# Four-layer, two-block forward pass: TensorE in source order at the norms, wider FFN opening tiles, urgent FFN adds, a norm mean in two steps

## Chip, cores and metric

One core of one Trainium2 chip runs the whole program. The time is the device time of one execution in microseconds (us); lower is better.

## What is computed

256 tokens of width 1024 go through a first block of two layers and a second block of two layers, all in float32. Written short, with the parts that the change touches:

```python
def mla_mixer(q_lat, kv_lat, k_rope, cos, sin, q_norm, kv_norm, w_uq, w_ukv, w_o):
    ...
    return o.reshape(bsz, s, MLA_WIDTH) @ w_o
def swiglu_ffn(h, w_gate_up, w_down):
    gt, up = jnp.split(h @ w_gate_up, 2, axis=-1)
    return (jax.nn.silu(gt) * up) @ w_down
def rmsnorm(x, g):
    y = x * lax.rsqrt(jnp.mean(x * x, axis=-1, keepdims=True) + 1e-6)
    return y * g
# first block, twice (l = 0, 1):
h = rmsnorm(x, norm_mix[l])
u, q_lat, kv_lat, k_rope, hq, hf, hi, hg, gate_logits = split(h @ w_in[l])
merged = sum over branches of sigmoid(gates[b]) * y_b      # b: s5, mla, hgrn2
x = x + merged @ w_out[l]
x = x + memory_cross_attention(rmsnorm(x, norm_cross[l]), rmsnorm(mem, norm_mem[l]), ...)
x = x + swiglu_ffn(rmsnorm(x, norm_ffn[l]), ffn_w_gate_up[l], ffn_w_down[l])
# then rmsnorm(x, norm_final), and the second block, twice:
y = concat(windowed_attention(...), rmsnorm(diff_attention(...), subln[l]))   # from rmsnorm(x, g_attn[l])
x = x + y @ w_out_2[l]
h = rmsnorm(x, g_ffn[l])
gate, val = split(h @ w_up_2[l]);  gate = conv3_over_tokens(gate)
x = x + (silu(gate) * val) @ w_down_2[l]
```

The FFN width is 2816, that is 22 pairs of 128 gate columns and 128 value columns. The MLA mixer has eight heads with keys of 96 rows (64 without and 32 with rotation).

## The kernel before

**Precision and weights.** Every product of float32 matrices is three matmuls: high times high, high times low and low times high part (`mm3`, lines 295 to 297). One such triple is called a step below. A weight tile of 128 by 1024 comes in by one 512 KB DMA on the SP queue into one of four raw buffers (`wload`, line 287), ACT copies its high part (`wh`, line 237), and DVE subtracts it from the raw tile to get the low part (`wl`, line 225).

**Who orders the work.** Each engine takes its instructions in one fixed order. The tile framework's scheduler makes that order from the source and from priorities: what stands under `urgent()` is put ahead of other work that is ready. `pe_order()` marks a stretch in which PE keeps the order of the source.

**Tokens and norms.** The 256 tokens are two tiles (t = 0, 1) of 128. The residual stream `x` is kept with tokens on partitions. A norm of class `Norm` runs per tile in this chain: the residual add of a PSUM half on DVE (line 225, `x<-x,ps`), the squares with their row sums on ACT (line 412, recorded at 237, `xs<-x`), after the second half the sum of both row sums on POOL (line 422), the mean on POOL (line 423), the power of minus one half on POOL (line 428), the scaling on DVE (line 234, `xs<-x,sm,g`, twice 512 columns), and then eight PE transposes (line 268, `ps<-con,xs`), whose results ACT and DVE split into the high and low part of `hh`, on which the next projection runs. `trans_split` (line 378) is the transposes with the split. The norms are the two of each layer's mixer and FFN, and the cross norm. `NormLate` and `Norm2` transpose the gained input before the root mean square is known, so that no transpose waits for the power.

**Projections.** `proj_a` keeps tokens on PSUM partitions; with `by_t` tile 0 is done wholly before tile 1. `proj_resid` adds a projection into the residual stream, then calls the next norm's squares and its power per tile. Where its weights have two k-groups (w_xo) it runs tile by tile and half by half, 12 matmuls of 512 columns for each.

**FFN** (`ffn`, line 1361). `head` (line 1376) does the first two gate/value pairs tile by tile: for each tile and pair 24 matmuls of 256 columns, 96 in an FFN. The other 20 pairs run with weights as the stationary operand and all 256 tokens moving: matmuls of 512 and 256 columns (`mm_both`, lines 378 to 381, `ps<-hh,wh`), then an ACT copy and a DVE add of the two PSUM halves (lines 1420 and 1421, recorded at 237 and 225, `UT<-ps,UT` and `MG<-ps,MG`). The down products of a pair follow three pairs later; the last four come tile by tile at the end, with the next norm's chain (lines 1428 to 1437).

**First mixer.** In layer 0 the constants of the S5 mixer are made beside the projections (`s5_prep`): DVE writes `PH` (line 225, `PH<-ST`), PE transposes it (line 268, `ps<-con,PH`), and ACT computes sines and exponentials, which need different tables (`ACT_TABLE_LOAD`). The FFN of layer 0 has the same preparation for layer 1 as its side work (on DVE `GT<-...`, `W<-...`, `Q<-...` and others, 896 columns).

**MLA scores.** `mla_attn` (line 1072) multiplies the rows 0 to 95 of `Q` and `K`.

## Time and profile before

| | |
|---|---|
| three runs | 1724.74, 1730.53, 1730.77 us, median 1730.53 us |
| the profiled execution | 1727.87 us, span 1725.8 us |
| TensorE clock granted over the span | 0.998 of full speed |
| PE | 1664.7 us busy (96 %), 9256 matmuls |
| DVE | 1326.3 us (77 %), 2474 instructions |
| ACT | 1008.1 us (58 %), 1790 instructions |
| POOL | 115.6 us (7 %), 174 instructions |
| chain that ended last | PE 73 %, DVE 11 %, ACT 8 %, issue 3 %, POOL 2 %, DMA 2 % |

The profiled execution lies 2.66 us under the median of the runs. In a row of the trace the first number is the start in us from the span's start, the second the duration; the name left of `<-` is written, the names right of it are read; the number in brackets is how long the engine was idle just before, and what ended that. Matmuls overlap, so that a row's duration is longer than the distance to the next one. A row with xN stands for N instructions of one form.

### The profile page before, as it was taken

What the parts mean: (1) busy time and instruction counts of PE and PEld (TensorE: products, weight loads), DVE (VectorE), ACT (ScalarE), POOL (GpSimd) and SP (SyncE); (2) the same over time, 40 slices, a digit from 0 to 9 for tenths busy, and PEclk for the clock granted to TensorE, in tenths of its full rate; (3) what the DMA queues carried; (4) which work ended last, traced back from release to release, by engine and by line L of the source; (5) the groups of instructions that cost most, each with busy time, mean ns of one, the idle gap of its engine ahead of it and who ended that gap; (6) DMA issues with size and microseconds to landing.
All of it is one profiled execution on the core that took longest, in us unless ns stands there. A gap on an engine that the chain in (4) does not pass through costs nothing.

```text
span 1725.8 us, 25598 instructions
## 1 busy us (share of the span) xinstructions
PE 1664.7 (96%) x9256; PEld 1386.3 (80%) x9256; DVE 1326.3 (77%) x2474; ACT 1008.1 (58%) x1790; POOL 115.6 (7%) x174
## 2 busy tenths in 40 slices
PE   7999999998999999999999999989899999999999
PEld 6977777887888788878778888866788886678887
DVE  7988887758976778975666666788687787878776
ACT  5873455556665576354465555657566655756554
POOL 1010000010110100000000000221000003100000
PEclk9999999999999999999999999999999999999999
DMA  7675464646677456446554666543466654346664
GB/s 238 186 262 166 155 209 146 186 150 188 221 254 239 142 165 187 154 148 189 186 172 162 188 194 192 167 147 113 135 190 190 193 169 145 110 131 187 190 190 133
DMA packets 85088, 304.92 MB, mean 177 GB/s; under 512 B 9569, under 2 KB 10337, under 8 KB 84961
## 3 DMA queue, kind: packets, MB, share of 16 engines
q1 hardware_dynamic: 81792, 291.74, 54.3%
q0 software_dynamic: 3168, 11.54, 1.9%
q8 instruction: 73, 1.20, 0.3%
q14 instruction: 55, 0.44, 0.1%
HBM read 290.66 MB, written 12.58 MB: 176 GB/s over the span
## 4 chain that ended last, share of the span: by engine, by line
PE 73%; DVE 11%; ACT 8%; issue 3%; POOL 2%; DMA 2%; SPq 0%; POOLq 0%; ACTq 0%; DVEq 0%
PE ps L379 17%; PE ps L295 13%; PE ps L297 13%; PE ps L296 13%; PE ps L378 7%; PE ps L268 3%; DVE wl L225 3%; ACT wh L237 3%; DVE W L225 2%; PE ps L1187 1%; ACT W L237 1%; PE ps L381 1%; PE ps L937 1%; PE ps L1072 1%; DVE W L949 1%
## 5 line engine op out<-in xcount | busy, mean ns | idle before, releaser
L225 DVE TENSOR_TENSOR wl<-wr,wh 128x1024 fp32r<-128x1024 f32 (+2 forms) x516 | 618.7, 1203 | 166.5 <-ACT wh L237 164.5
L237 ACT ACTIVATE wh<-wr 128x1024 fp32r<-128x1024 f32 (+2 forms) x516 | 536.1, 1042 | 310.8 <-PE ps L297 203.7
L379 PE MATMUL ps<-hh,wh 128*128 128x512 f32 x1280 | 450.4, 397 | 2.9 <-DVE UT L225 2.7
L378 PE MATMUL ps<-hh,wl 128*128 128x256 f32 x1120 | 312.5, 279 | 0.7 <-DVE wl L225 0.7
L379 PEld LDWEIGHTS ps<-hh,wh 128*128 128x128 f32 x1280 | 234.4, 188 | 49.6 <-issue 3.2
L295 PE MATMUL ps<-wh,hh 128*128 128x512 f32 (+2 forms) x640 | 233.7, 367 | 4.2 <-ACT UT L237 3.9
L296 PE MATMUL ps<-wl,hh 128*128 128x512 f32 (+2 forms) x640 | 235.1, 368 | 2.3 <-DVE wl L225 2.2
L297 PE MATMUL ps<-wh,hh 128*128 128x512 f32 (+2 forms) x640 | 232.8, 364 | 0.0
L378 PEld LDWEIGHTS ps<-hh,wl 128*128 128x128 f32 x1120 | 211.2, 189 | 8.0 <-DVE wl L225 1.0
L295 PEld LDWEIGHTS ps<-wh,hh 128*128 128x128 f32 x640 | 121.4, 190 | 23.8 <-ACT UT L237 4.4
L296 PEld LDWEIGHTS ps<-wl,hh 128*128 128x128 f32 x640 | 121.6, 190 | 22.8 <-DVE wl L225 4.5
L297 PEld LDWEIGHTS ps<-wh,hh 128*128 128x128 f32 x640 | 121.7, 190 | 17.3 <-issue 1.0
L295 PE MATMUL ps<-wh,PH 128*128 128x512 f32 x256 | 101.0, 396 | 2.2 <-ACT PH L237 1.7
L296 PE MATMUL ps<-wl,PH 128*128 128x512 f32 x256 | 101.0, 396 | 0.4 <-DVE wl L225 0.4
L297 PE MATMUL ps<-wh,PL 128*128 128x512 f32 x256 | 100.0, 392 | 0.0
L295 PE MATMUL ps<-wh,OH 128*128 128x512 f32 x208 | 83.2, 400 | 0.0
L296 PE MATMUL ps<-wl,OH 128*128 128x512 f32 x208 | 82.8, 398 | 0.0
L297 PE MATMUL ps<-wh,OL 128*128 128x512 f32 x208 | 82.4, 397 | 0.0
L237 ACT ACTIVATE UT<-ps 128x256 f32<-128x256 f32 (+2 forms) x120 | 46.5, 389 | 53.5 <-PE ps L379 51.6
L237 ACT ACTIVATE MG<-ps 128x256 f32<-128x256 f32 (+1 forms) x84 | 31.7, 377 | 47.4 <-PE ps L379 47.2
L268 PE MATMUL ps<-con,xs 128*128 128x128 f32 x232 | 36.9, 289 | 22.8 <-DVE xs L234 19.6
L295 PEld LDWEIGHTS ps<-wh,PH 128*128 128x128 f32 x256 | 47.9, 188 | 12.9 <-ACT PH L237 2.7
(450 smaller groups left out, 2976.6 us busy)
## 6 DMA issues: line engine op xcount, KB each, us to landing
wr<-in_w_gu SPq DMA_DIRECT2D x176, 512.0 KB, 4.5
wr<-in_w_dn SPq DMA_DIRECT2D x88, 512.0 KB, 3.6
wr<-in_w_gt SPq DMA_DIRECT2D x48, 512.0 KB, 3.9
wr<-in_w_out SPq DMA_DIRECT2D x32, 512.0 KB, 3.9
wr<-in_w_b SPq DMA_DIRECT2D x24, 512.0 KB, 4.0
s5w<-sw SPq DMA_DIRECT2D x16, 704.0 KB, 5.2
wr<-in_w_glu SPq DMA_DIRECT2D x16, 512.0 KB, 4.1
g<-in_gains SPq DMA_DIRECT2D x12, 512.0 KB, 4.9
```

Source lines behind the costliest of these rows:

```text
L225: V.tensor_tensor(out=o, in0=x, in1=y, op=op)
L237: S.activation(out=o, in_=x, func=f, **k)
L268: T.transpose(o, x_, ident[0:k, 0:k])
L295: T.matmul(ps, lhsT=ah, rhs=bh, start=start, stop=False)
L296: T.matmul(ps, lhsT=ah, rhs=bl, start=False, stop=False)
L297: T.matmul(ps, lhsT=al, rhs=bh, start=False, stop=stop)
L378: T.matmul(ps[:, 0], lhsT=wl_, rhs=xx.hi(kt), start=False, stop=False)
L379: T.matmul(ps, lhsT=wh_, rhs=xx.both[kt], start=first, stop=last)
L381: T.matmul(ps[:, 0], lhsT=wl_, rhs=xx.hi(kt), start=False, stop=False)
L937: T.matmul(bu[:, jj, k, :], lhsT=bT[:, k, jj, :], rhs=u2[:, p, :], start=True, stop=True)
L949: V.tensor_tensor_scan(out=z, data0=rb, data1=z, initial=0.0, op0=MUL, op1=ADD)
L1072: T.matmul(s[:, e, :], lhsT=qT[0:96, h, t * P : (t + 1) * P], rhs=kT[0:96, h, 0 : P * (t + 1)], start=True, stop=False,)
```

## The change

Five parts:

1. `joint()` opens a stretch in which PE keeps the source's order, at the end of every `proj_resid` and of every FFN but the last; `joint_end()` closes it after the first tile of the next projection (`ends=True`, or in the FFN head). In such a stretch the transposes of a norm are put off (`defer`) and issued after a counted number of steps (`tick`): 6 for the first half and 7 for the second of a `Norm`, 4 for the late norms, or before a matmul that needs them (`need`).
2. The opening two pairs of each FFN are one tile 512 columns wide: 48 matmuls of 512 columns in place of 96 of 256. Their four weight loads of 512 KB are packed two k-tiles by 512 columns. The copy of the head's result is urgent.
3. The ACT copy and the DVE add behind each later pair are urgent.
4. The mean takes one POOL instruction behind the second half's squares in place of two: the first half's row sum is scaled before (`part`). In the very first norm both stay behind.
5. The MLA scores run over 128 rows in place of 96; POOL clears rows 96 to 127 of `Q` and `K` first (two memsets of 32 by 2048 in a layer of the first block).

The DVE instructions are the same; ACT has four more table loads (13 in place of 9).

```diff
-    o["w_gu"] = _pack(_pairs(i["ffn_w_gate_up"], FT), 4, 256)
+    for k, n in (("w_gu", "ffn_w_gate_up"), ("w_gu2", "w_up_2")):
+        w = _pairs(i[n], FT)
+        o[k + "h"] = _pack(w[:, :, : 256 * HEAD], 2, 256 * HEAD)[:, 0]
+        o[k] = _pack(w[:, :, 256 * HEAD :], 4, 256)
...
                 c0 = j * step + col
+                xx.need(t, k0 + j)
                 mm3(
...
                 )
+                tick()
...
-        def proj_a(src, nk, n, xx, evac, by_t=False):
+        late_tr, region = [], []
+        def joint():
+            region.append(pe_order())
+            region[-1].__enter__()
+        def joint_end():
+            if region:
+                while late_tr:
+                    late_tr.pop(0)[2]()
+                region.pop().__exit__(None, None, None)
+        def defer(key, steps, fn):
+            if region:
+                late_tr.append([key, steps, fn])
+            else:
+                fn()
+        def tick():
+            for e in late_tr:
+                e[1] -= 1
+            while late_tr and late_tr[0][1] <= 0:
+                late_tr.pop(0)[2]()
+        def needed(keys):
+            while any(e[0] in keys for e in late_tr):
+                late_tr.pop(0)[2]()
+        def proj_a(src, nk, n, xx, evac, by_t=False, ends=False):
...
                     gemm_a(us, xx, t, pss[t])
+                    if ends:
+                        joint_end()
                     with urgent():
...
-            def mean(self, ss, add=EPS):
+                if c == 0 and self.row:
+                    self.part(self.ss[t])
+            def part(self, ss, add=EPS):
+                G.tensor_scalar(out=ss[:, 0:1], in0=ss[:, 0:1], scalar1=1.0 / D, scalar2=add, op0=MUL, op1=ADD)
+            def mean(self, ss):
+                if not self.row:
+                    self.part(ss)
                 m = small(1)
-                G.tensor_tensor(out=m, in0=ss[:, 0:1], in1=ss[:, 1:2], op=ADD)
-                G.tensor_scalar(out=m, in0=m, scalar1=1.0 / D, scalar2=add, op0=MUL, op1=ADD)
+                G.tensor_scalar(out=m, in0=ss[:, 1:2], scalar1=1.0 / D, scalar2=ss[:, 0:1], op0=MUL, op1=ADD)
                 return m
...
-                    trans_split(xs, 4, *self.h[0:2], 4 * c, t)
+                    self.turn(t, c, xs, 6 + c)
...
+            def turn(self, t, c, xs, steps):
+                def f():
+                    with urgent():
+                        trans_split(xs, 4, *self.h[0:2], 4 * c, t)
...
+                defer((self.row, t, c), steps, f)
...
+            def need(self, t, kt):
+                needed([(self.row, u, kt // 4) for u in ((0, 1) if t is None else (t,))])
...
-                return _X(*([z[:, k] for k in range(8)] for z in (hi, lo, h)))
+                return _X(*([z[:, k] for k in range(8)] for z in (hi, lo, h)), self.need)
...
+            add = EPS
...
                 act(junk, self.src(t, c), AF.Square, accum_out=self.ss[t][:, c : c + 1])
+                if c == 0:
+                    self.part(self.ss[t], self.add)
...
             if inner:
+                joint()
                 acc = [[mm_([P, 512]) for c in range(2)] for t in range(2)]
...
                 us = [units(src[c], 2, 512) for c in range(2)]
+                joint()
                 for t in range(2):
...
             proj_a(src[0], 2, 512, xx, done(0))
+            joint()
             proj_a(src[1], 2, 512, xx, done(1), by_t=True)
...
-            proj_a(a["w_ql"][l, 0], 2, 512, xx, ev_q, by_t=True)
+            proj_a(a["w_ql"][l, 0], 2, 512, xx, ev_q, by_t=True, ends=True)
...
             kT = slot("K", [P, 8, 256])
+            for z in (qT, kT):
+                G.memset(z[96:128], 0.0)
             for g in range(2):
...
-                            s[:, e, :], lhsT=qT[0:96, h, t * P : (t + 1) * P], rhs=kT[0:96, h, 0 : P * (t + 1)],
+                            s[:, e, :], lhsT=qT[:, h, t * P : (t + 1) * P], rhs=kT[:, h, 0 : P * (t + 1)],
...
-            def head(n):
...
-                us = [units(src_gu[j], 4, 256) for j in range(n)]
-                gu = slot("K", [P, 2, n, 2, P])
+            def head():
...
+                us = units(src_h, 2, 256 * HEAD)
+                gu = slot("K", [P, 2, HEAD, 2, P])
...
-                    ps = ax([P, n, 256])
-                    for j in range(n):
-                        gemm_a(us[j], hx, t, ps[:, j])
-                    cp(gu[:, t], ps)
+                    ps = ax([P, 256 * HEAD])
+                    gemm_a(us, hx, t, ps)
+                    joint_end()
+                    with urgent():
+                        cp(gu[:, t].rearrange("p j c n -> p (j c n)"), ps)
...
                                 )
-                            cp(sums[:, c], ps[c][:, 1])
-                            tt(sums[:, c], ps[c][:, 0], sums[:, c], ADD)
+                            with urgent():
+                                cp(sums[:, c], ps[c][:, 1])
+                                tt(sums[:, c], ps[c][:, 0], sums[:, c], ADD)
                     middle(j, sums[:, 0], sums[:, 1], hi[:, j % 4, :], lo[:, j % 4, :])
...
                         down(jj, (0, 1), (0, 1))
+            if not isinstance(nxt, Store):
+                joint()
             for t in range(2):
...
                         down(jj, (t,), (c,))
+                        tick()
                     with urgent():
```

**PE at the norm ahead of the first FFN's head.** `xs` is the scaled tile (3787 before, 3794 now, both tile 0); `ps_3826`, `ps_3843` before and `ps_3819`, `ps_3837` now are the two halves of tile 1 of w_xo. Before:

```order
L297 MATMUL ps_3826<-wh_3754,PL_3691 128x512
L295 MATMUL ps_3826<-wh_3754,PH_3690 128x512
L296 MATMUL ps_3826<-wl_3755,PH_3690 128x512
L297 MATMUL ps_3826<-wh_3754,PL_3691 128x512
L268 MATMUL ps_3811<-con,xs_3787 128x128 x4
L295 MATMUL ps_3843<-wh_3760,PH_3690 128x512
L268 MATMUL ps_3819<-con,xs_3787 128x128 x4
L296 MATMUL ps_3843<-wl_3761,PH_3690 128x512
L297 MATMUL ps_3843<-wh_3760,PL_3691 128x512
```

Now:

```order
L298 MATMUL ps_3837<-wh_3765,PH_3695 128x512
L299 MATMUL ps_3837<-wl_3766,PH_3695 128x512
L300 MATMUL ps_3837<-wh_3765,PL_3696 128x512
L271 MATMUL ps_3844<-con,xs_3794 128x128 x4
L298 MATMUL ps_3837<-wh_3771,PH_3695 128x512
L299 MATMUL ps_3837<-wl_3772,PH_3695 128x512
L300 MATMUL ps_3837<-wh_3771,PL_3696 128x512
L271 MATMUL ps_3854<-con,xs_3794 128x128 x4
L298 MATMUL ps_3837<-wh_3771,PH_3695 128x512
L299 MATMUL ps_3837<-wl_3772,PH_3695 128x512
L300 MATMUL ps_3837<-wh_3771,PL_3696 128x512
```

The first transposes stood behind the 12 matmuls of tile 1's first half; now they stand behind 18 matmuls, the second four 3 further. For tile 1 they stood behind 30 head matmuls of 256 columns, and now stand behind 18 of 512.

**DVE in the first FFN, at the add of the first pair that ends beside side work.** `UT` is the pair's sum, `GT`, `W`, `Q` and `s5...` are the side work. Before:

```order
L234 SCALAR_TENSOR_TENSOR PL_4297<-B_845_4352,PH_4296 128x256
L225 TENSOR_TENSOR GT_818_4210<-ST_793_4094,ST_794_4095 128x8x112
L225 TENSOR_TENSOR W_820_4212<-ST_794_4095,ST_793_4094 128x896
L225 TENSOR_TENSOR wl_4551<-wr_4548,wh_4550 128x1024
L225 TENSOR_TENSOR GT_818_4210<-GT_818_4210,W_820_4212 128x8x112
L225 TENSOR_TENSOR UT_4396<-ps_4394,UT_4396 128x256
L225 TENSOR_TENSOR UT_4396<-ps_4395,UT_4396 128x256
L225 TENSOR_TENSOR Q_4209<-ST_794_4095 128x8x112
```

Now:

```order
L228 TENSOR_TENSOR s5cr_4159<-s5q_813_4153,s5q_814_4154 128x16
L228 TENSOR_TENSOR W_820_4172<-ST_793_4054 128x896
L228 TENSOR_TENSOR UT_4356<-ps_4354,UT_4356 128x256
L228 TENSOR_TENSOR s5cr_4159<-s5cr_4159,s5d_4152 128x16
L228 TENSOR_TENSOR s5q_813_4153<-s5im_4083,K_3968 128x16
L228 TENSOR_TENSOR s5q_814_4154<-s5re_4082,K_3968 128x16
L228 TENSOR_TENSOR Q_4169<-ST_794_4055 128x8x112
L228 TENSOR_TENSOR s5ci_4160<-s5q_813_4153,s5q_814_4154 128x16
L237 SCALAR_TENSOR_TENSOR B_845_4312<-B_845_4312,MG_844_4272 128x256
L228 TENSOR_TENSOR wl_4434<-wr_4431,wh_4433 128x1024
L228 TENSOR_TENSOR UT_4356<-ps_4355,UT_4356 128x256
L228 TENSOR_TENSOR wl_4488<-wr_4485,wh_4487 128x1024
```

The two adds stood together behind three passes of 896 columns (`GT`, `W`, `GT`) and two splits; now those three passes come behind both adds, and one pass of 896 columns (`Q`), a split and smaller side work stand between the two.

**PE in the first mixer, at the first transpose of PH.** `hh` is the normed input. Before the rows belong to w_hi:

```order
L295 MATMUL ps_1628<-wh_1605,hh_117 128x512
L296 MATMUL ps_1628<-wl_1606,hh_117 128x512
L297 MATMUL ps_1628<-wh_1605,hh_117 128x512
L295 MATMUL ps_1627<-wh_1611,hh_117 128x512
L296 MATMUL ps_1627<-wl_1612,hh_117 128x512
L297 MATMUL ps_1627<-wh_1611,hh_117 128x512
L295 MATMUL ps_1627<-wh_1611,hh_117 128x512
L268 MATMUL ps_1021<-con,PH_950 128x128
L296 MATMUL ps_1627<-wl_1612,hh_117 128x512
L297 MATMUL ps_1627<-wh_1611,hh_117 128x512
L295 MATMUL ps_1628<-wh_1611,hh_117 128x512
```

Now they belong to the second half of w_hf:

```order
L299 MATMUL ps_1411<-hh_117,wh_1401 128x256
L300 MATMUL ps_1411<-hh_117,wl_1402 128x256
L298 MATMUL ps_1411<-hh_117,wh_1401 128x256
L299 MATMUL ps_1411<-hh_117,wh_1401 128x256
L300 MATMUL ps_1411<-hh_117,wl_1402 128x256
L298 MATMUL ps_1411<-hh_117,wh_1401 128x256
L271 MATMUL ps_1023<-con,PH_952 128x128
L299 MATMUL ps_1411<-hh_117,wh_1401 128x256
L300 MATMUL ps_1411<-hh_117,wl_1402 128x256
L298 MATMUL ps_1411<-hh_117,wh_1401 128x256
L299 MATMUL ps_1411<-hh_117,wh_1401 128x256
```

The transpose moved ahead of 137 matmuls of 256 columns (the rest of w_hf and w_hq) and 16 of 512 (w_hi). DVE's write of this part of `PH` moved too, ahead of eight splits, six passes and a memset of 1024 columns on `GT` and `W`, four passes `B` and two `YL`.

At the start of the program, ACT casts the first two weight tiles ahead of the squares of the second token tile (before: behind them), and DVE makes the low part of the first weight tile ahead of the scaling of the first token tile, and of the second ahead of that of the second (before: both scalings first).

## Rows read from the trace of the kernel before

**Rows 1.** Page, busy time, share and instructions of each engine.

```profile
PE 1664.7 (96%) x9256; PEld 1386.3 (80%) x9256; DVE 1326.3 (77%) x2474; ACT 1008.1 (58%) x1790; POOL 115.6 (7%) x174
```

**Rows 2.** Waits of PE: us in total, times, longest.

```profile
PE ps L268 <- DVE xs L234: 19.6, 15, 7.7
```

**Rows 3.** Timeline, layer 0, norm ahead of the FFN, tile 0.

```profile
366.56 0.39 PE L297 MATMUL ps<-wh,PL 128*128 128x512 f32 x1
...
366.98 0.69 DVE L225 TENSOR_TENSOR x<-x,ps 128x512 f32<-128x512 f32 x1 [1.81 <-PE ps L297]
...
367.70 0.63 ACT L237 ACTIVATE xs<-x 128x512 f32<-128x512 f32 x1 [1.71 <-DVE x L225]
...
368.57 0.19 POOL L422 TENSOR_TENSOR sm<-sm 128x1 f32<-128x1 f32 x1 [4.50 <-ACT xs L237]
...
368.85 0.19 POOL L423 TENSOR_SCALAR sm<-sm 128x1 f32<-128x1 f32 x1
...
369.27 0.39 PE L297 MATMUL ps<-wh,PL 128*128 128x512 f32 x1
...
369.72 1.41 DVE L234 SCALAR_TENSOR_TENSOR xs<-x,sm,g 128x512 f32<-128x512 f32 x2 [2.05 <-POOL sm L428]
...
370.62 0.63 PE L268 MATMUL ps<-con,xs 128*128 128x128 f32 x4 [0.95 <-DVE xs L234]
```

**Rows 4.** Timeline, the same norm, tile 1, PE alone.

```profile
374.07 0.39 PE L297 MATMUL ps<-wh,PL 128*128 128x512 f32 x1
...
374.31 0.27 PE L295 MATMUL ps<-wh,hh 128*128 128x256 f32 x1
...
377.77 0.28 PE L297 MATMUL ps<-wh,hh 128*128 128x256 f32 x1
...
378.86 0.66 PE L268 MATMUL ps<-con,xs 128*128 128x128 f32 x4 [0.81 <-DVE xs L234]
```

**Rows 5.** Timeline, waits of the same kind elsewhere: start, and inner norms.

```profile
11.67 1.97 PE L268 MATMUL ps<-con,xs 128*128 128x128 f32 x8 [2.01 <-DVE xs L234]
...
37.34 0.44 PE L268 MATMUL ps<-con,xs 128*128 128x128 f32 x2 [1.01 <-DVE xs L234]
...
600.15 0.41 PE L268 MATMUL ps<-con,xs 128*128 128x128 f32 x2 [0.56 <-DVE xs L234]
```

**Rows 6.** Timeline, first FFN, a pair that waits for its add.

```profile
426.98 0.39 PE L297 MATMUL ps<-wh,OL 128*128 128x512 f32 x1
...
428.45 1.08 DVE L225 TENSOR_TENSOR GT<-GT,W 128x896 f32<-128x896 f32 x1
...
430.02 0.47 PE L379 MATMUL ps<-hh,wh 128*128 128x512 f32 x1 [2.65 <-DVE UT L225]
```

**Rows 7.** Timeline, start of the program.

```profile
9.59 1.06 ACT L237 ACTIVATE wh<-wr 128x1024 fp32r<-128x1024 f32 x1
...
12.79 1.22 DVE L225 TENSOR_TENSOR wl<-wr,wh 128x1024 fp32r<-128x1024 f32 x1
...
26.11 0.39 PE L297 MATMUL ps<-wh,hh 128*128 128x512 f32 x1
```

**Rows 8.** Timeline, first mixer, first transpose of PH.

```profile
95.82 0.42 DVE L225 TENSOR_TENSOR PH<-ST 64x256 f32<-64x256 f32 x1
...
96.30 0.33 PE L268 MATMUL ps<-con,PH 128*128 128x128 f32 x1 [1.43 <-DVE PH L225]
```

**Rows 9.** Timeline, first mixer, a table load and what follows it.

```profile
74.53 1.28 ACT L237 ACT_TABLE_LOAD   x1
...
75.83 0.60 ACT L237 ACTIVATE xs<-ps 128x512 f32<-128x512 f32 x1
```

**Rows 10.** Busy time by window, first mixer (us, PE, PEld, DVE, ACT, POOL).

```profile
69.00:94.00 25.00, 25.00 (x194) 24.21 (x194) 22.74 (x42) 18.50 (x25) 1.77 (x2) 1.00 0.65 207
```

**Rows 11.** Groups by line and form: memsets on POOL of 128 by 2048.

```profile
L1524 POOL MEMSET Q<- 128x2048 f32 x2 | 3.6, 1810 | 119.2 <-PE ps L268 93.2 <-PE ps L1620 26.0
```

**Rows 12.** MLA scores, line 1072: durations in ns, minimum, median, maximum.

```profile
L1072 PE MATMUL ps<-K,Q x64: 275/377/634, 65.3 to 659.3; 96*128 96x128 f32 x32, 96*128 96x256 f32 x32
```

More of the change, by code (lines that the diff above doesn't have):

```diff
@@ L31 @@
 FT = 22
+HEAD = 2
 EPS = 1e-6
@@ L97, in _layout @@
     o["w_out2"] = _pack(w, 2, 512)
-    o["w_gu2"] = _pack(_pairs(i["w_up_2"], FT), 4, 256)
     o["w_dn2"] = _pack(i["w_down_2"], 1, 1024)
@@ L161, with __init__ @@
 class _X:
-    def __init__(self, his, los, both=None):
-        self.his, self.los, self.both = his, los, both
+    def __init__(self, his, los, both=None, need=lambda t, kt: None):
+        self.his, self.los, self.both, self.need = his, los, both, need
     def hi(self, kt):
@@ L336, in proj_b @@
             ks = [(u, j) for u in us for j in range(nk)]
+            for u, j in ks:
+                xx.need(None, u[2] + j)
             with pe_order():
@@ L456, in gained @@
                 tt(self.xs[t][:, c, :], self.src(t, c), self.g[:, c * 512 : (c + 1) * 512], MUL)
-                trans_split(self.xs[t][:, c, :], 4, *self.h[0:2], 4 * c, t)
+                self.turn(t, c, self.xs[t][:, c, :], 4)
             def squares(self, t, c):
@@ L476, in two_block_kernel @@
         class Norm2(NormLate):
+            add = 0.0
             def __init__(self, row0, row):
@@ L501, in squares @@
                 act(junk, x_, AF.Square, accum_out=self.s2[t][:, c : c + 1])
+                if c == 0:
+                    self.part(self.s2[t])
             def __call__(self, t):
                 self.m1[t] = self.mean(self.s2[t])
-                m2, q = self.mean(self.ss[t], 0.0), small(1)
+                m2, q = self.mean(self.ss[t]), small(1)
                 G.tensor_scalar(out=q, in0=self.m1[t], scalar1=EPS, scalar2=None, op0=MUL)
@@ L1335, in ev_q @@
                     tt(p, p, bc(ri, 256), MUL)
-            proj_a(a["w_xq"][l, 0], 2, 512, cx, ev_q, by_t=True)
+            proj_a(a["w_xq"][l, 0], 2, 512, cx, ev_q, by_t=True, ends=True)
             proj_a(a["w_xv"][l, 0], 2, 512, mx, lambda t, pv: cp(v[:, t, :], pv))
@@ L1358, in layer1, with ffn @@
             return nf
-        def ffn(src_gu, src_dn, hx, middle, nxt, side=iter(())):
+        def ffn(src_h, src_gu, src_dn, hx, middle, nxt, side=iter(())):
             acc = [[mm_([P, 512]) for c in range(2)] for t in range(2)]
@@ L1394, in ffn @@
             dn = {}
-            LAG, HEAD = 3, 2
-            gu = head(HEAD)
+            LAG = 3
+            gu = head()
             for j in range(FT + LAG):
@@ L1407, in ffn @@
                 elif j < FT:
-                    us = units(src_gu[j], 4, 256)
+                    us = units(src_gu[j - HEAD], 4, 256)
                     ps = [ax([P, 2, 256]) for c in range(2)]
@@ L1557, in ev_kva @@
                 ev(1, 2)(t, ps)
-            proj_a(a["w_qa2"][l, 0], 2, 512, hx, ev(0, 8, True), by_t=True)
+            proj_a(a["w_qa2"][l, 0], 2, 512, hx, ev(0, 8, True), by_t=True, ends=True)
             proj_a(a["w_kva2"][l, 0], 2, 256, hx, ev_kva)
@@ L1663, in layer2 @@
             proj_resid(a["w_out2"][l], mkx((yah, yal, 4), (ybh, ybl, 4)), nxt_ffn, True)
-            ffn(a["w_gu2"][l], a["w_dn2"][l, 0], nxt_ffn.X(), convglu(l), nxt)
+            ffn(a["w_gu2h"][l], a["w_gu2"][l], a["w_dn2"][l, 0], nxt_ffn.X(), convglu(l), nxt)
         nx = Norm(0)
@@ L1696, in two_block_kernel @@
             )
-            ffn(a["w_gu"][l], a["w_dn"][l, 0], nf.X(), swiglu, nx, side)
+            ffn(a["w_guh"][l], a["w_gu"][l], a["w_dn"][l, 0], nf.X(), swiglu, nx, side)
             nbank["ax"] = 4
```

## The prediction, made before the changed kernel was run

> **What bounds the kernel now.** I read the page's busy times first: PE is busy for 96 % of the span [rows 1], so that there are two ways to gain, fewer PE cycles or fewer of the gaps in which PE waits. The view of waits tells which gaps: the largest single kind is the transposes of a norm that wait for the scaled tile, 19.6 us in 15 waits [rows 2]. The timeline of one such norm shows why [rows 3]. The last matmul of tile 0 starts at 366.56; then come, one behind the other, the residual add on DVE (366.98), the squares on ACT (367.70), three small POOL instructions (368.57 to 369.69), the scaling on DVE (369.72), and the first transpose at 370.62. PE had 12 matmuls to do meanwhile, the last at 369.27, and then sat idle for 0.95 us. Tile 1 looks the same with 30 head matmuls as cover and 0.81 us idle [rows 4]. The reader should see that the chain is a little longer than the cover, by under a microsecond each time.
>
> Five of the 15 waits are of another sort: two at the start of the program (7.7, the longest wait of [rows 2], and 2.01) and three in inner norms of the MLA front (1.01, 0.52 and 0.56, together 2.09; the first and the last of the three stand in [rows 5]). The other ten are eight at the four FFN heads and two at the end of the first FFN: 19.6 - 7.7 - 2.01 - 2.09 = 7.8 us idle.
>
> **Norm stalls, -9.2 us.** A matmul of 512 columns costs (369.27 - 366.56) / 12 = 0.226 us [rows 3], one of 256 columns (377.77 - 374.31) / 29 = 0.119 us [rows 4]. From start to start, the stall costs more than its idle time: 370.62 - 369.27 = 1.35, less 0.23 of the matmul itself, is 1.12 us for tile 0, and 1.09 - 0.12 = 0.97 for tile 1, 2.09 us for 1.76 idle. On 7.8 us idle that makes 9.2 us. The chain from the end of the last matmul (366.56 + 0.39) to the transpose is 3.67 us. One POOL instruction fewer takes 0.28 us off it (368.57 to 368.85), leaving 3.39. The new cover is 18 matmuls, 18 x 0.226 = 4.07 us from the same point: no stall, 0.7 us to spare. For tile 1 the chain is 378.86 - 374.46 = 4.40, less 0.28 is 4.12, against the same 4.07: no margin, but a stall of at most 0.1. It was longer because a weight split stood ahead of the residual add on DVE. I take the whole 9.2. Ends: 4.6, if tile 1 keeps its stall at every norm, and 11.3, if the three inner waits went too. The late norms and the cross norms lose no such time now, so that putting PE in source order there gains nothing; a transpose that is only moved costs the same.
>
> The trace says 0.226 us for a matmul of 512 columns, and the cover rests on that. The Trainium skill, page "TensorE: Matmul & The Clock Gate", section "Back-to-back issue gap", gives about 131 ns as the sustained spacing at 512 columns. By that figure 18 matmuls would cover 2.4 us, a stall of about 1 us would stay at each norm, and this term would be near 0; the rows of this case, at a granted clock of full speed, do not agree with it.
>
> **The urgent adds, -2.8 us.** In the first FFN a pair's matmul waits 2.65 us for the add `UT`, because DVE does side work of 896 columns first, the last pass at 428.45 [rows 6]. From start to start it is 430.02 - 426.98 = 3.04, less 0.23: 2.8 us. The new order has those passes behind both adds, with one pass (1.08 us) and a split left between the two. What is late next is the side work, which has the rest of the FFN as its cover. Ends: 0, if the wait only moves to a later split, and 2.8.
>
> **The head's width, -2.3 us.** 96 x 0.119 = 11.42 us become 48 x 0.226 = 10.85 [rows 3, 4], 0.57 us in each of four FFNs, 2.3 in all; 0 is the other end. The weights are the same four loads of 512 KB on the SP queue in the same place, and the splits the same four.
>
> **The start, +1.8 us.** ACT now casts two weight tiles before the second token tile's squares, and DVE makes the first low part before it scales tile 0. The first raw tile is cast at 9.59 [rows 7], until 10.65; the split takes 1.22, until 11.87; then the scaling (0.7), the eight transposes (1.97) [rows 5] and a cast and a split of `hh` of 0.6 and 0.7 bring the first full step to about 15.9. 48 matmuls of 0.226 (10.8) and the second tile's transposes (1.2) end w_ql at 27.9, where the last one now starts at 26.11. An estimate: +1.8, with ends 0 (the casts wait less than I think) and 3.6 (both casts and splits lie on the path of tile 1 too).
>
> **The first mixer, +2.0 us.** PE now meets the first transpose of PH ahead of 137 matmuls of 256 and 16 of 512 columns, 137 x 0.119 + 16 x 0.226 = 19.9 us of work earlier. Today it waits 1.43 us, for a DVE write that ends at 96.24 [rows 8]. That write moved too: ahead of eight splits (8 x 1.22 = 9.8 us) [rows 7] and seven passes of 1024 columns (7.6 us at the 1.08 of a pass of 896) [rows 6], with the small ones some 18 us. So PE comes 20 earlier and the data 18 earlier: the wait of 1.4 grows to about 3.4, +2.0. Ends: -1.4, if the wait goes, and +18, if the data comes no earlier than now.
>
> **Edits at nothing.** Four more table loads on ACT, 1.28 us each [rows 9], are 5.1 us; all four fall in the first mixer, where ACT is busy for 18.5 of 25 us [rows 10], so that 6.5 us are free for them. The cover is thin: gone, it is +5.1. The memsets of `Q` and `K` are 1.8 us each on POOL [rows 11], which is 7 % busy [rows 1]; the ones of layer 0 stand in the idle start. They delay only POOL's own queue. Scores over 128 rows: a matmul of 256 columns over 128 rows lasts 0.27 [rows 4], over 96 rows 0.28 to 0.63 [rows 12], so that rows cost nothing; 64 matmuls x 0 to 0.02.
>
> **Sum.** -9.2 - 2.8 - 2.3 + 1.8 + 2.0 = -10.5 us. The working is against the profiled execution's 1727.87 us, which lies 2.66 us under the median of the three runs. Set against the median, 1730.53 - 10.5 = **1720.0 us**. A measurement of this kernel can tell 0.5 % from no change, 8.65 us: faster means under 1721.9, slower over 1739.2.
>
> **Rivals.**
> *Deeper gain.* Source order and urgent adds also shorten splits that now keep PE waiting, and the first mixer costs nothing: -11.3 - 2.8 - 2.3 + 0 - 1.4 = -17.8, 1713 us. For it: PE still has some gaps of other kinds. Against it: the work on DVE stays the same.
> *Cover lost.* Tile 1 has no margin. If a weight split of 1.22 us still gets ahead of the residual add, tile 1 stalls as before and the norms give 4.6, and if the urgent adds push a split behind, those 2.8 are given back: -4.6 - 2.3 + 1.8 + 2.0 = -3.1, 1727 us. For it: [rows 4] show just that, and DVE is 77 % busy.
> *Table loads bind.* Each new load is on PE's path: -10.5 + 5.1 = -5.4, 1725 us. For it: loads fall between casts that PE needs. The row shows the next instruction 0.02 us behind the load's end [rows 9]. The Trainium skill, page "ScalarE: Activation LUTs", section "What ACT_TABLE_LOAD costs", adds a drain of 1.38 us and gives 2.66 us for a switch; four would be an estimate of 10.6 us and the time 1731. The trace does not agree, the 1.28 us stand alone.
> *The first mixer binds (slower).* DVE's write of PH needs ACT's results (sines, exponentials), which this change delays with its table loads; if it ends at 96.2 as now, PE stands 18 us longer at the transpose. With the loads on the path: -9.2 - 2.8 - 2.3 + 1.8 + 18 + 5.1 = +10.6, 1741 us. It decides from the point where the mixer and start cost over 14.3 + 8.7 = 23 us. Against it: the order has the write itself 18 us of DVE work earlier.
> *It does not do what it says.* The scheduler could place the chain's DVE steps late just as before. The order shows the transposes moved, so that this is left inside the second rival.
>
> **How the numbers follow.** My forecast, 1715 to 1727, 0.53, of which 0.33 lies under 1721.9 (its middle is only 1.9 us below that bound); deeper gain 0.13; cover lost 0.15; table loads 0.07; first mixer 0.12, of which 0.02 ends within 0.5 %. Together faster 0.33 + 0.13 = 0.46, slower 0.10, the same 0.44. The range takes the deeper gain whole and stops short of the worst mixer: 1711 to 1737; left out are a tenth above and less below.
>
> **What would show it.** Right: the waits of the transposes for the scaled tile fall from 15 to about five; the first FFN has no wait for `UT`; the last w_ql matmul stands near 28; PE waits some 3 us at the first PH. Wrong: a wait of over 0.5 us at tile 1 of each FFN norm (the second rival), or a gap of over 10 us on PE between 70 and 100 us (the fourth).

## The result, and the profile of the changed kernel

The change made the kernel slower: 1742.52 us median (1738.49 to 1744.39, 5 runs) against 1730.53 us before, ratio 1.0076 with a 95 % interval of 1.0054 to 1.0098. The forecast was 1720.0 us with a range of 1711 to 1737, and faster; the time lies outside the range, on the other side. The profiled execution has a span of 1739.2 us against 1725.8, 13.4 us more.

Two readings of the changed kernel's trace already say that this is not the forecast with a wrong size. In busy time by engine, which answers to [rows 1]:

```profile
PE 1668.9 (96%) x9064; PEld 1377.7 (79%) x9064; DVE 1320.4 (76%) x2474; ACT 1014.8 (58%) x1794; POOL 131.0 (8%) x178
```

192 matmuls fewer, as the wider head says, and yet PE is busy for 4.2 us more. So matmuls took longer, or overlapped less; the clock rows below show one reason. And in the view of PE's waits (us in total, times, longest), which answers to [rows 2]:

```profile
PE ps L271 <- DVE xs L237: 15.0, 6, 12.9
PE ps L271 <- DVE C L228: 5.0, 3, 2.1
PE ps L298 <- ACT hh L240: 4.7, 9, 0.8
PE ps L299 <- DVE wl L228: 4.1, 5, 1.7
...
PE ps L417 <- DVE wl L228: 2.7, 3, 1.9
```

The transposes' wait for the scaled tile did fall from 15 to 6 times, just as the order promised. But the longest of them, the one at the program's start, grew from 7.7 to 12.9 us, a new line has come, matmuls that wait for the cast of `hh` (nine times, seven of them at the heads), and the wait for the low part of a weight (L299) is up from 2.6 us before to 4.1.

Where the 13.4 us arose is read by taking the same instruction in both traces. Before, the first transpose starts at 7.69 us; now at 12.93. The table gives, for such marks, the start before and by how much it is later (+) or earlier (-) in the changed kernel and in four of the experiments below.

| mark on PE | before | change | run 1: no part 5 | run 2: before + part 5 | run 4: run 1, late norms free | run 5: parts 2 to 4 |
|---|---|---|---|---|---|---|
| first transpose | 7.69 | +5.24 | -0.06 | +5.22 | -0.05 | -0.12 |
| layer 0, first matmul of the S5 mixer | 132.18 | +10.45 | -0.44 | +11.27 | +0.31 | -0.43 |
| layer 0, cross attention's output | 356.56 | +6.61 | -0.36 | +8.92 | -1.16 | +0.69 |
| first FFN, pair 2 | 390.31 | +6.47 | -0.84 | +8.83 | -1.65 | -1.23 |
| first FFN, pair 7 | 433.61 | +2.94 | -4.32 | +8.79 | -5.13 | -4.75 |
| first FFN, pair 12 | 475.36 | +7.26 | -3.84 | +9.06 | -4.66 | -4.21 |
| layer 1, cross attention's output | 904.22 | +8.25 | -2.92 | +8.68 | -3.83 | -4.76 |
| second FFN, last pair | 1096.91 | +7.86 | -3.32 | +8.68 | -4.24 | -5.65 |
| third FFN, pair 2 | 1243.14 | +13.36 | +2.33 | +8.36 | -1.61 | -5.39 |
| last matmul | 1721.72 | +13.44 | +3.36 | +8.25 | -2.76 | -6.72 |

Three losses and one gain are plain in the third column: +6.6 in the first 357 us (start and first mixer), -3.5 at pair 7 (the urgent adds), +4.3 from pair 7 to pair 12, and +5.5 between the second and the third FFN. The heads, on which the forecast's largest term rested, show next to nothing: from the cross attention's output to pair 2 the first FFN takes 33.6 us in place of 33.7, the second 30.7 in place of 31.2, and the wider head alone was priced at 0.6 in each.

A column is one execution, so small differences between columns are no reading. Runs 4 and 6 have the same order on all engines up to 373 us, and are 2.7 us apart at the cross attention's output; 1.7 us of that is a stretch of lower clock that only one of the two traces has there. And at the S5 mark the changed kernel has done 775 matmuls, the kernel before 758, so that part of the +10.45 is work moved ahead; at the cross attention's output both have done 1958.

**The start.** The timeline of the changed kernel's first 31 us:

```profile
0.72 1.80 POOL L1087 MEMSET Q<- 32x2048 f32 x1 [0.29 <-POOLq L1788]
...
2.46 1.80 POOL L1087 MEMSET K<- 32x2048 f32 x1
...
6.28 0.56 POOL L474 TENSOR_TENSOR sm<-sm,nhalf 128x1 f32<-128x1 f32 x1
9.90 1.06 ACT L240 ACTIVATE wh<-wr 128x1024 fp32r<-128x1024 f32 x1 [4.15 <-DMA wr<-in_w_ql]
10.99 1.23 DVE L228 TENSOR_TENSOR wl<-wr,wh 128x1024 fp32r<-128x1024 f32 x1 [4.47 <-ACT wh L240]
...
12.13 1.41 DVE L237 SCALAR_TENSOR_TENSOR xs<-x,sm,g 128x512 f32<-128x512 f32 x2
...
12.93 1.99 PE L271 MATMUL ps<-con,xs 128*128 128x128 f32 x8 [12.93 <-DVE xs L237]
...
16.29 2.21 PE L271 MATMUL ps<-con,xs 128*128 128x128 f32 x8 [0.31 <-DVE xs L237]
...
18.72 0.63 PE L300 MATMUL ps<-wh,hh 128*128 128x512 f32 x1
19.14 0.63 PE L298 MATMUL ps<-wh,hh 128*128 128x512 f32 x1
...
30.99 0.39 PE L300 MATMUL ps<-wh,hh 128*128 128x512 f32 x1
```

The memsets are over at 4.26 us and keep nobody waiting on the chip: the power of tile 0 is done at 6.84 us, about when it was before. But DVE then sits for 4.47 us in front of a weight split, because in its fixed order the split stands ahead of the scaling, and the split waits for ACT's cast, which waits for a DMA.

**The first FFN, pairs 7 to 12.** Rows of POOL and ACT, and the wait on PE that they end in:

```profile
455.34 1.81 POOL L1087 MEMSET Q<- 32x2048 f32 x1 [5.86 <-DMA sw<-Q]
...
457.20 0.53 POOL L887 MEMSET ST<- 128x512 f32 x1
...
457.77 0.84 ACT L240 ACTIVATE ST<-raw 64x256 f32<-64x256 f32 x2 [3.81 <-POOL ST L887]
458.63 1.06 ACT L240 ACTIVATE wh<-wr 128x1024 fp32r<-128x1024 f32 x1
...
465.71 0.57 PE L417 MATMUL ps<-hh,wl 128*128 128x256 f32 x1 [1.94 <-DVE wl L228]
```

Layer 1's memset of `Q` is issued early on POOL and must wait until a DMA has read the old `Q`. Behind it in POOL's queue stands the clearing of `ST`, for which ACT waits 3.81 us, and behind ACT's copies stand the weight casts.

**The norm ahead of the first FFN**, where [rows 3, 4] showed waits of 0.95 and 0.81 us:

```profile
377.53 0.60 PE L271 MATMUL ps<-con,xs 128*128 128x128 f32 x4
...
378.58 0.63 ACT L240 ACTIVATE xs<-x 128x512 f32<-128x512 f32 x1 [1.11 <-DVE x L228]
...
379.21 1.04 ACT L240 ACTIVATE wh<-wr 128x1024 fp32r<-128x1024 f32 x1
...
380.16 1.07 ACT L240 ACTIVATE hh<-ps 128x512 fp32r<-128x512 f32 x2
...
380.79 0.50 PE L298 MATMUL ps<-wh,hh 128*128 128x512 f32 x1 [0.84 <-ACT hh L240]
...
387.19 0.50 PE L299 MATMUL ps<-wl,hh 128*128 128x512 f32 x1 [0.85 <-DVE wl L228]
...
389.73 0.50 PE L298 MATMUL ps<-wh,hh 128*128 128x512 f32 x1 [0.69 <-ACT K L240]
```

The first transposes no longer wait. What they produce is not cast before 380.16, behind the next squares and a weight cast on ACT, and the head's first matmul waits for it: 0.84 us in place of 0.95. In tile 1 it is 0.85 for a weight split, in place of 0.81, and 0.69 more behind it.

**The late norm behind the second FFN**, and the granted clock there (per window: length, then busy us and count of PE, PEld, DVE, ACT, POOL, then the granted clock as a share of full speed):

```profile
1119.54 0.63 PE L271 MATMUL ps<-con,xs 128*128 128x128 f32 x4 [1.40 <-DVE xs L228]
1121.39 0.79 PE L298 MATMUL ps<-wh,hh 128*128 128x512 f32 x1 [0.59 <-ACT hh L240]
1142.84 0.63 PE L271 MATMUL ps<-con,C 128*128 128x128 f32 x4 [2.14 <-DVE C L228]
1144.90 0.72 PE L298 MATMUL ps<-wh,hh 128*128 128x512 f32 x1 [1.43 <-ACT UT L240]
```

```profile
465.00:470.00 5.00, 4.29 (x16) 3.73 (x17) 4.97 (x9) 1.99 (x4) 0.00 (x0) 0.66 0.59 175
1120.00:1125.00 5.00, 4.29 (x12) 3.04 (x11) 4.73 (x6) 5.00 (x10) 0.61 (x1) 0.66 0.37 105
1145.00:1150.00 5.00, 4.99 (x15) 3.45 (x16) 3.22 (x20) 1.01 (x4) 2.35 (x5) 0.66 0.72 247
```

Before, no transpose waited there for the gained tile: PE waited for three weight splits of under 0.6 us, then 1.56 us for `UT`. Now it waits 1.40 us for the gained tile, 0.59 for its cast, 2.14 for `C` and 1.43 for `UT`. Three times, each behind such waits (1.94, 1.40 and 0.59, 2.14 and 1.43 us), the mean granted clock of a 5 us window is 0.66, so the lower of the two levels, 1.2 GHz, holds for about 0.34 / 0.5 x 5 = 3.4 us, and the work of 1.7 us is lost. In all windows of 5 us the trace of before has the like twice, near 130 and 1440 us. That is where the longer matmuls come from, in part. From the second FFN's last pair to pair 2 of the third, where the changed kernel loses 5.5 us, all waits of PE sum to 10.7 us before and 12.6 now: 1.9 us of the loss are waits, 3.4 are two of these stretches of lower clock.

### The profile page after: what moved, and what is told of

Read it like the earlier page. It is cut to its first block, busy times and chain, and to the rows that moved or that the text cites. A ratio compares the mean times of both kernels' runs of the same rounds, so it can differ in the third digit from the quotient of the medians.

```text
span 1739.2 us, 25097 instructions
## 1 busy us (share of the span) xinstructions
PE 1668.9 (96%) x9064; PEld 1377.7 (79%) x9064; DVE 1320.4 (76%) x2474; ACT 1014.8 (58%) x1794; POOL 131.0 (8%) x178
## 3 DMA queue, kind: packets, MB, share of 16 engines
q8 instruction: 71, 1.16, 0.3%
## 4 chain that ended last, share of the span: by engine, by line
PE 71%; DVE 11%; ACT 8%; issue 4%; DMA 3%; POOL 3%; SPq 0%; ACTq 0%; POOLq 0%; DVEq 0%
PE ps L418 16%; PE ps L298 13%; PE ps L300 13%; PE ps L299 13%; PE ps L417 7%; DVE wl L228 3%; PE ps L271 3%; ACT wh L240 2%; PE ps L1256 1%; DVE W L228 1%; ACT W L240 1%; PE ps L420 1%; PE ps L1004 1%; POOL sm L395 1%; DVE sm L729 1%
## 5 line engine op out<-in xcount | busy, mean ns | idle before, releaser
L298 PE MATMUL ps<-wh,hh 128*128 128x512 f32 (+2 forms) x576 | 226.6, 394 | 9.1 <-ACT hh L240 4.7
L299 PE MATMUL ps<-wl,hh 128*128 128x512 f32 (+2 forms) x576 | 223.6, 389 | 3.8 <-DVE wl L228 3.7
L300 PE MATMUL ps<-wh,hh 128*128 128x512 f32 (+2 forms) x576 | 222.6, 387 | 0.0
L298 PEld LDWEIGHTS ps<-wh,hh 128*128 128x128 f32 x576 | 109.8, 191 | 32.8 <-ACT hh L240 8.0
L299 PEld LDWEIGHTS ps<-wl,hh 128*128 128x128 f32 x576 | 109.9, 191 | 26.2 <-DVE wl L228 5.9
L300 PEld LDWEIGHTS ps<-wh,hh 128*128 128x128 f32 x576 | 109.7, 191 | 23.5 <-issue 2.6
L299 PE MATMUL ps<-wl,PH 128*128 128x512 f32 x256 | 100.3, 392 | 0.0
L299 PE MATMUL ps<-wl,OH 128*128 128x512 f32 x208 | 83.4, 401 | 0.0
L299 PEld LDWEIGHTS ps<-wl,PH 128*128 128x128 f32 x256 | 48.1, 188 | 10.2 <-DVE wl L228 0.7
```

The source lines that it names most:

```text
L298: T.matmul(ps, lhsT=ah, rhs=bh, start=start, stop=False)
L299: T.matmul(ps, lhsT=ah, rhs=bl, start=False, stop=False)
L300: T.matmul(ps, lhsT=al, rhs=bh, start=False, stop=stop)
```

## The experiments

All twelve compute the whole output. Times are medians; the kernel before, run on the same chip, had 1728.92 us for runs 1 to 4, 1728.95 for runs 5 to 8, and 1729.16 for runs 9 to 12.

**Run 1, the change without part 5.**

```diff
-            for z in (qT, kT):
-                G.memset(z[96:128], 0.0)
...
-  lhsT=qT[:, h, t * P : (t + 1) * P], rhs=kT[:, h, 0 : P * (t + 1)],
+  lhsT=qT[0:96, h, t * P : (t + 1) * P], rhs=kT[0:96, h, 0 : P * (t + 1)],
```

> The changed kernel without its fifth part: no memsets of Q and K, scores over 96 rows. Theory M (the two memsets at the head of POOL's queue change the scheduler's order of the start and of the first mixer, and the later memset of Q, which waits for a DMA, holds up POOL's queue in the first FFN): the start gives back about 4 us, the first mixer about 2.6, the first FFN about 4.5 of 1742.5, so about 1731. Rival J (the source order of PE at the norms is what costs, the memsets are beside other work): at least 1739.

Measured: 1732.37 us (1730.24 to 1734.67), ratio to before 1.0023 (1.0013 to 1.0033). That is 10 us under the change (9 by the two ratios to the kernel before); theory M had said about 1731 us, rival J at least 1739. In the table the start is back to -0.06, the first mixer to -0.36, and the loss between pairs 7 and 12 shrinks from 4.3 to 0.5. ACT's table loads are back at nine.

**Run 2, before with part 5 alone.** The same lines, added to the kernel before.

> The kernel before with the memsets and the scores over 128 rows alone. Theory M: 1730.5 + 4 + 2.6, and up to 4.5 more if the side work of the first FFN waits too, so 1737 to 1742, and the first transpose of the program near 12.9 us in place of 7.7. Rival J: 1731, as before.

Measured: 1737.60 us, ratio 1.0046 (1.0029 to 1.0064). The first transpose, and the table loads:

```profile
12.92 0.47 PE L268 MATMUL ps<-con,xs 128*128 128x128 f32 x1 [12.92 <-DVE xs L234]
```

```profile
L237 ACT ACT_TABLE_LOAD x13 | 16.7, 1283 | 0.9 <-PEq L1716 0.7
```

So the late start, the new order of the first mixer and the four extra table loads all come with part 5 and with nothing else of the change: up to 329 us PE, ACT and DVE have the order of the changed kernel here. The first FFN loses only 0.2 between pairs 2 and 12: the memset of `Q` blocks POOL at a harmful moment only together with another part. The urgent adds, which put the side work off, are the likely one; no run has these two alone.

**Run 3, before with the urgent adds alone.**

```diff
-                            cp(sums[:, c], ps[c][:, 1])
-                            tt(sums[:, c], ps[c][:, 0], sums[:, c], ADD)
+                            with urgent():
+                                cp(sums[:, c], ps[c][:, 1])
+                                tt(sums[:, c], ps[c][:, 0], sums[:, c], ADD)
```

> The kernel before with the FFN copies and adds urgent, alone. If the adds were what kept PE waiting in the first FFN: 1727 to 1728 and no wait of the matmuls for UT. If the side work that is put off pays it back as waits for a weight split: 1730 to 1732.

Measured: 1725.01 us, ratio 0.9979 (0.9970 to 0.9988), 3.9 us less. The wait of the matmuls for `UT` [rows 6] is gone from the list of waits, and is not paid back in the first FFN. It gains somewhat more than the 2.8 forecast, though 1.6 us of the 4.3 at pair 12 are lost again behind the second FFN. There the transposes of the late norm now wait 1.92 us for the gained tile (at 1107.05 us), which they did not before, and a stretch of lower clock worth 1.7 us follows.

**Run 4, run 1 with the late norms left free.**

```diff
-            if not isinstance(nxt, Store):
+            if type(nxt) is Norm:
                 joint()
```

> As the first of these runs, and PE's source order not at the ends of those FFNs that a late norm follows (second FFN and third). Theory L (the fixed order there costs the second block's first mixer some 6 us: a wait of 1.4 and 0.6 us at the gained tile, a slower granted clock behind it, and later waits): 4 to 6 us under the first run, about 1726. Rival (that mixer's new order comes from somewhere else): the same time as the first run within 1 us.

Measured: 1725.86 us (1724.58 to 1727.43), ratio 0.9983 (0.9974 to 0.9992), 6.5 us under run 1. From the second FFN's end to the third FFN it loses 2.6 us, run 1 5.7. Theory L holds in its time: the fixed order at the late norms is the second loss. Its account holds in part. PE's waits in that stretch sum to 12.9 us in run 1 and 10.5 in run 4; the one for `C` falls from 2.14 to 0.42, but the one for the gained tile stays, at 1.63 us, as in run 3, where PE is not in source order. The lower clock stays too: 6.8 us of it stand in both traces, in run 4 from 1210 us.

**Run 5, parts 2 to 4 alone.** `joint()` does nothing, so that the transposes are issued with the scaling, as before, and part 5 is out; they keep an `urgent()` of their own, which run 12 takes out.

```diff
         def joint():
-            region.append(pe_order())
-            region[-1].__enter__()
+            pass
```

> The changed kernel without the first part's source order (transposes are issued where the scaling stands, as before) and without the fifth. Theory N (the source order only moves the norm wait: from the transposes that wait for the scaled tile to the head's matmuls that wait for the cast of hh): no slower than the fourth run, 1722 to 1726. Rival (the source order is worth the 9.2 us of the norm stalls and other parts lose them): 1730 or more.

Measured: 1722.28 us (1719.74 to 1724.14), ratio 0.9950 (0.9932 to 0.9968). It is 3.6 us under run 4: source order at the other norms costs too, it does not gain. Theory N holds in its time. Part of the cost is at the heads: from the cross attention's output to pair 2 run 4 takes 33.3 us in the first FFN and 30.7 in the second, run 5 takes 31.8 and 30.2, with no lower clock in either. The rest is not located.

**Run 6, run 4 with the deferred transposes and their casts more urgent** (`with urgent(5000)` in `turn`).

> The fourth run's kernel with the deferred transposes, and so the cast and split of hh behind them, at double urgency, ahead of the weight casts. If ACT's order (squares and weight casts ahead of the cast of hh) is what leaves the head waiting: the waits of the matmuls for hh, 4.7 us in nine, mostly go, 2 to 4 us under the fourth run, about 1723. If the weight split is what comes last then: the same within 1 us, or slower.

Measured: 1728.89 us, ratio 0.9998 (0.9987 to 1.0010), 3.0 us over run 4. The waits for `hh` are what they were (3.5 us in seven, in both), and the orders of PE, ACT and POOL are those of run 4 throughout. Only DVE's order changed, from the first FFN's norm on, where the split of `hh` now stands ahead of a residual add. So this run says nothing on what ACT's order costs, and neither of its two theories was tested; why it is slower stays open.

**Run 7, before with the wider head alone** (part 2 without its urgent copy).

> The kernel before with the wider opening tile alone. By the price of 0.57 us in each FFN: 2.3 us under the kernel before, 1726.6. If the first head matmul now waits for a weight tile that carries two k-tiles of both pairs: 1729 to 1731.

Measured: 1725.87 us, ratio 0.9971 (0.9957 to 0.9984), 3.1 us less by the medians and 5.0 by the ratio; 2.3 were expected.

**Run 8, before with the mean in two steps alone** (part 4).

> The kernel before with the mean in two steps alone. If one POOL instruction of 0.28 us is off the chain of each of the ten norm waits: 10 x 0.28 = 2.8 us less, about 1726. If DVE is busy with a weight split when the scaling is released, or POOL's new instruction gets in the way: no change, 1729.

Measured: 1726.76 us, ratio 0.9981 (0.9970 to 0.9993), 2.2 us less; 2.8 were expected.

**Run 9, before with the memsets alone, scores over 96 rows** (the two added lines of part 5).

> The kernel before with the two memsets per layer alone, scores still over 96 rows. Theory M: the same as the second run, 1737.6 within 1 us, first transpose near 12.9 us. Rival (the scores over 128 rows cost, or pay): 2 us or more away from it.

Measured: 1738.00 us, ratio 1.0053 (1.0032 to 1.0074), and the first transpose at 12.79 us. Run 2 is within 0.4 us of it: the memsets are the whole of part 5's cost; the 128 rows cost nothing that these runs can tell.

**Run 10, the change with the clearing bound to `hh`.** Rows 96 to 127 become zero times a part of `hh`.

```diff
-                G.memset(z[96:128], 0.0)
+                h_ = hall[96:128, 0:4].bitcast(F32).rearrange("p a b c -> p (a b c)")
+                G.tensor_scalar(out=z[96:128].rearrange("p a b -> p (a b)"), in0=h_,
+                                scalar1=0.0, scalar2=0.0, op0=MUL, op1=ADD)
```

> The changed kernel whole, but rows 96 to 127 of Q and K are cleared by multiplying a part of the layer's hh by zero, so that the clearing can't come before hh is there: it is the same size on POOL, but not at the head of its queue. Theory M, in the form that only the place counts: 1732 to 1733, as the first run, which has no clearing at all. Rival (the 1.8 us passes on POOL, or the 128 rows, cost wherever they stand): 1737 or more.

Measured: 1734.32 us (1729.94 to 1737.83), ratio 1.0033 (1.0020 to 1.0047): between the two theories, nearer to M. Its first transpose is back at 7.51 us, but at the S5 mixer it is 6.2 us late again. The trace shows a new cause, in POOL's clearings and in DVE's next three splits:

```profile
15.97 1.91 POOL L1088 TENSOR_SCALAR Q<-hh 32x2048 f32<-32x2048 f32 x1 [4.54 <-DVE hh L228]
16.33 6.91 DVE L228 TENSOR_TENSOR wl<-wr,wh 128x1024 fp32r<-128x1024 f32 x3
17.94 2.78 POOL L1088 TENSOR_SCALAR K<-hh 32x2048 f32<-32x2048 f32 x1
...
18.87 2.92 DVE L228 TENSOR_TENSOR wl<-wr,wh 128x1024 fp32r<-128x1024 f32 x1
```

Three splits take 6.91 us where one takes 1.22 [rows 7]; the last row is the second of them by itself. PE waits 0.69 and 1.20 us for such splits. PE and ACT keep the order of run 1, so that the 6.2 us are not a changed order; where the rest of them comes from was not followed. So the place at the head of POOL's queue is what spoils the start, but this substitute brought a cost of its own, and the run does not say what a clearing without it would give.

**Run 11, run 4 with the transposes two steps earlier** (`4 + c` in place of `6 + c`).

> The fourth run's kernel with the transposes of a norm counted two steps (six matmuls, 1.36 us) earlier: after 4 and 5 steps in place of 6 and 7. If the transposes stood too late for the cast of hh that the head needs: the waits of the matmuls for hh go, waits of the transposes for the scaled tile of up to 0.7 us come back, 1724 to 1726. If ACT's order decides and not the place of the transposes: the hh waits stay and the others come on top, 1728 to 1731.

Measured: 1727.99 us, ratio 1.0002 (0.9989 to 1.0016), 2.1 us over run 4. PE's waits in run 4, then in run 11, then in run 5:

```profile
PE ps L271 <- DVE xs L237: 11.3, 5, 7.6
PE ps L299 <- DVE wl L228: 4.8, 6, 1.7
...
PE ps L298 <- ACT hh L240: 3.5, 7, 0.6
```

```profile
PE ps L271 <- DVE xs L237: 22.3, 15, 7.6
...
PE ps L299 <- DVE wl L228: 2.0, 4, 0.9
```

```profile
PE ps L271 <- DVE xs L237: 17.5, 15, 7.6
...
PE ps L299 <- DVE wl L228: 1.7, 3, 0.8
```

The waits for `hh` vanish and those for the scaled tile return, from 5 to 15, as the first theory said, but at up to 1.5 us each, and the time misses its 1724 to 1726. Set later, the transposes make PE wait behind them; set earlier, ahead of them. The sum of these waits is 19.6 us in run 4, 24.3 in run 11, and 19.2 in run 5, whose transposes stand where the scheduler puts them and whose mean is the shorter one too. The whole kernel is fastest in run 5, by more than these waits differ from run 4's.

**Run 12, run 5 without the urgency around the transposes.**

> The fifth run's kernel without the urgency around the transposes and the cast and split of hh: wider head, urgent adds and copies, mean in two steps, norms else as before. By the sum of the three parts measured alone (1725.0, 1725.9 and 1726.8 against 1728.9, so -3.9, -3.1 and -2.2): 1719.7. If the fifth run's nested urgency did nothing: 1722.3 within 1 us.

Measured: 1721.59 us (1718.17 to 1723.69), ratio 0.9963 (0.9951 to 0.9976). The intervals of runs 5 and 12 overlap, so which of the two is faster is not settled; both beat the kernel before and the change. The three parts alone gave -3.9, -3.1 and -2.2; together -6.7 (run 5) and -7.6 (run 12), not -9.2. By the ratios it is -3.6, -5.0 and -3.3 alone, -8.6 and -6.4 together, each with an interval of 2 to 3 us to either side, so that the shortfall is not firm.

## Why the prediction was wrong, by its own steps

**The memsets, "edits at nothing": failed, and this is the largest miss.** The step was "the ones of layer 0 stand in the idle start. They delay only POOL's own queue". On the chip that is true of the start, where they end before POOL is needed. But what I priced was their execution, and what they changed was the order: with two passes of 1.8 us ready at the head of POOL's queue, the scheduler placed ACT's and DVE's weight work ahead of the norm's. That the memsets do it is shown (runs 1, 2 and 9); what the scheduler reckoned with is not. Runs 2 and 9 put it at 8.7 and 8.8 us on the kernel before, run 1 at 10.2 on the change, which has the wait in the first FFN as well. I had seen both symptoms in the order, the casts at the start and the moved `PH` transposes, and given them terms of their own (+1.8 and +2.0) without asking which part made them. With that question run 1's kernel would have been the thing to look at, since its order at the start is the old one. And for layer 1 I did not ask what stands behind the memset in POOL's queue: ACT waits 3.81 us for it.

**The start, +1.8: path right, size off.** The first transposes were put at about 12.6 by its working and came at 12.93. But the last matmul of w_ql came at 30.99 in place of 27.9: tile 1's squares now stand behind two casts, and its transposes came at 16.29 us and not inside the matmuls of tile 0. The working also took 0.226 us for each of the 48 matmuls, where those from 18.14 to 21.70 us stand 0.43 us apart. The upper end was 3.6, measured are 4.9.

**The first mixer, +2.0: failed in its mechanism.** Start and first mixer together were forecast at +3.8 and are +6.6, 1.7 of it in the mixer; in runs 2 and 9, which have the same order there, the mixer is at +4.6 and +4.9, with a stretch of lower clock worth 1.7 us that the trace before has too and the change's has not. So that 1.7 comes near the 2.0 forecast is luck. The forecast wait of some 3 us at the first transpose of `PH` is not there (at 78.51 us PE does not wait); PE waits 1.18 us for `PL`, 1.68 and 1.14 for `C`, 0.88 for a split, and 2.18 at the S5 mixer's first matmul, as before (2.13). The 18 us of the slower rival never occurred. That rival gave 1741 us, close to the 1742.5 measured, but for a reason that the trace does not show: that it met the time is chance.

**The norm stalls, -9.2: failed.** "The new cover is 18 matmuls, 18 x 0.226 = 4.07 us from the same point: no stall, 0.7 us to spare." The cover ahead of the transposes was right. What I left out is that the transposed tile must be cast and split before the head's first matmul, and that six matmuls later there is nothing else for PE to do. The chain is one from the residual add to the first head matmul, some 24 matmuls of cover in all, and moving the transposes inside it only chooses at which of the two places PE waits, as runs 4 and 11 show. Not even that comes free: without source order the kernel is 3.6 us faster (run 5). The -2.8 of the shorter mean is real by itself (run 8: -2.2).

**"The late norms and the cross norms lose no such time now, so that putting PE in source order there gains nothing": failed by its sign.** It costs: without it run 4 is 6.5 us faster. In source order PE stands still where the scheduler had put other matmuls (12.9 us of waits in place of 10.5). That PE waits for the gained tile at all is not the source order's doing, since the wait stands in runs 3, 4 and 5 too; it came with the urgent adds (run 3).

**The urgent adds and the head's width: right.** -2.8 and -2.3 were forecast, -3.9 and -3.1 measured alone. The first FFN has no wait for `UT`, as forecast. The table loads at nothing: they are four more as forecast, and leave with part 5; what they alone cost was not tried.

The stated sign that would prove me wrong, "a wait of over 0.5 us at tile 1 of each FFN norm", did occur at the first FFN (0.85 and 0.69 us) but not at the other three (0.45 to 0.46 us), and the rival that it belonged to had it from DVE ahead of the transposes.

Added up from run 5, by the medians: 1722.3, 3.6 more for source order at the other norms (run 4), 6.5 for the late norms (run 1), 10.2 for part 5, and that is the 1742.5 of the change. Of part 5, runs 2 and 9 put 4.3 and 4.7 us at the start (last matmul of w_ql at 30.42 and 30.83 in place of 26.11) and the rest in the first mixer.

What stays open: which waits make up the mixer's share; where source order costs the rest of its 3.6 us; whether ACT's cast order alone could save the norm waits (run 6 did not change that order); and whether runs 12 and 5 truly gain less than their parts.

## What to carry to other kernels

An instruction that an idle engine does for nothing still has a price where a scheduler orders the others around it: when the order changes in places that an edit doesn't speak of, find the part that moved it before pricing the rest. A wait that is filled from before must be followed to the next instruction that uses the result: cover counted on one side of the transposes was taken from the other. And a fixed order is worth putting only where PE waits now; where a scheduler has already filled the gap, it opens one.

## What the runs showed of the hardware

DVE's splits, two inputs from SBUF, took 2.62, 2.92 and 1.52 us beside POOL instructions that read SBUF (run 10), against 1.22 us alone, and each ends 1.07 to 1.09 us behind the end of the POOL instruction beside it (17.88, 20.72 and 22.15 us). Beside a POOL memset, which reads nothing, splits keep their duration: in the changed kernel two at 453.91 us took 2.37 us, with the memset of `Q` starting at 455.34. The Trainium skill, page "SBUF — State Buffer", section "SBUF: two separate sides", says that the two engines lock one pair of ports against each other for a whole instruction, and of a DVE instruction with two SBUF inputs that it happens only against a POOL instruction that reads SBUF. The rows of run 10 and of that memset agree. Small instructions can be held up too: the mean of tile 1 took 0.93 us on POOL at 382.99 us of the changed kernel, beside a split, where its median is 0.265.

A gap on PE of 1.4 to 2.1 us can cost more than itself: three times in the changed kernel about 1.7 us of work were lost to a lower granted clock behind it. Other gaps of that length, such as the 2.18 us at 142.63 us, had no such window behind them. PE's order does not decide it alone: runs 4 and 6 have the same one throughout, and, apart from the very end, run 4's trace has one stretch at the lower level, 6.8 us from 1210 us, run 6's four of 3.4 us, at 134, 1134, 1212 and 1441 us. What decides it these runs do not show.
